# Memory attention with its factors made ahead: one token pipeline, and neighbourhood columns moved between the mLSTM

## The chip, the cores and the metric

The kernel runs on one core of a Trainium2 chip. The metric is the device time of one execution in microseconds; the median of several runs is given. The engines are named as the profile names them: PE (TensorE, matmuls), PEld (its weight loads), DVE (VectorE), ACT (ScalarE), POOL (GpSimd) and SP (SyncE, whose queue issues nearly all DMAs here).

## The reference, cut to what matters

One encoder layer over 1024 tokens of width 1024. Three sub-layers follow each other, each as x <- LayerNorm(alpha * x + f(x)): a token mixer (a bidirectional mLSTM with 4 heads of 128 beside a neighbourhood attention with 8 heads of 64), a cross-attention into 256 memory tokens, and a gated convolutional FFN. The change is in the cross-attention and in where the work around it stands.

```python
def memory_xattn(x, mem, w_q, w_kv, w_o, b_o):
    q = (x @ w_q).reshape(b, t, XA_HEADS, XA_DIM)          # 4 heads of 256
    k, v = jnp.split(mem @ w_kv, 2, axis=-1)               # each reshaped to (b, 256, 4, 256)
    s = jnp.einsum('bthd,bmhd->bhtm', q, k) * (XA_DIM ** -0.5)
    p = jax.nn.softmax(s, axis=-1)
    o = jnp.einsum('bhtm,bmhd->bthd', p, v).reshape(b, t, d)
    return o @ w_o + b_o
```

All inputs and outputs are fp32, and `w_q`, `w_kv`, `w_o` are 1024 rows deep.

## The kernel before, in words

**Precision.** A product is made of three matmuls (`mm3`, lines 220 to 222): each operand is a pair of a high part and a remainder, and high x high, high x low and low x high are summed in PSUM. Pairs are in fp32r (`wload`, `split`) in the mixer and in f16 with a power-of-two scale (`wload16`, `split16`, lines 196 and 197) from the cross-attention on. A weight comes by DMA into a `wraw` tile (two buffers), ACT makes `whi` from it, DVE or POOL makes `wlo` (five buffers each). The scales come from surveys of the weights and from bounds that are worked out on the chip.

**Order.** All engines run their own instruction streams. A tile framework orders each stream at build time, by program order and by its own simulated clock, and puts in the waits. A tile of a pool takes a buffer when an earlier tile of the same tag is free; pools that are opened after others were closed take over their memory. `mix(tc, anchor, main, total, fill, ftotal, lag)` interleaves two generators: after each step of `main` it takes steps of `fill`, in proportion, and holds them on each engine behind an instruction of `main` that is `lag` steps back.

**Stages.** (1) Tokens: eight tiles of x are normalized, transposed into `xT` (X1 for tokens 0 to 511, X2 for the rest) and multiplied with the token-major weights (`tok_chunk`); eight surveys of `w_xo` and `w_xq` run beside. (2) Columns: sixteen columns of `w_col`, each for both halves of the tokens, 32 groups of 24 matmuls (bank `cl`): q and k of the mLSTM, then q and k of the neighbourhood attention (stored to `nqk_d`). The gate scan and the backward state pass of the mLSTM run beside. (3) mLSTM (`ml_gen`), chunk by chunk; its fill is `mem_gen`: sixteen groups of 24 matmuls that make K (`xk_d`) and V (`xv_d`) of the 256 memory tokens. (4) Neighbourhood attention (`na_gen`), with the first half of the output product as its fill (`out_a`). The mLSTM's result `yml` lies in X1. (5) The second half of the output product (`out_half` with `after1`): norm, and `to_h1`, which transposes the normalized tile, applies the norm's weight and bias per partition and splits it into f16; POOL applies them to the row-major tile, which goes to `h1_d`. (6) The query projection `xq_gen` (16 groups of 24 matmuls; each column of `w_xq` is loaded and split twice, once for each half of the tokens) and the attention `attn` by head and half, with `load_kv` reading K and V back; the query projection is the fill. (7) `attn` goes on with the output product `out_d` as its fill; `w_xo` is loaded and split as `wD`. (8) The last four tiles of `out_d`, with the first units of the FFN being prepared (`units.bound`, `scale`, `prep`), and `to_B`, which makes the FFN's operands. (9) The FFN, then the down-projection.

## Time and profile before

| what | us |
|---|---|
| median of 3 runs (1615.37 to 1618.26) | 1616.17 |
| the profiled execution | 1614.52 |
| its span, first to last instruction | 1612.8 |
| PE busy in the span | 1500.4 |
| DVE busy | 1003.2 |
| ACT busy | 765.5 |
| POOL busy | 552.8 |

The mean granted clock of PE over the span is 0.976 of full speed. A row of a group reads: line, engine, operation, names of what is written and read, tile of the matmul, shape and type written and read, count, then busy time and mean of one in ns, then idle time of the engine just before and what ended it. PE's instructions overlap each other in the pipeline, so their busy times add up to more than the time they need; the distance from one start to the next is the pace.

### The profile page before, as it was taken

What the parts mean: (1) busy time and instruction counts of PE and PEld (TensorE: products, weight loads), DVE (VectorE), ACT (ScalarE), POOL (GpSimd) and SP (SyncE); (2) the same over time, 40 slices, a digit from 0 to 9 for tenths busy, and PEclk for the clock granted to TensorE, in tenths of its full rate; (3) what the DMA queues carried; (4) which work ended last, traced back from release to release, by engine and by line L of the source; (5) the groups of instructions that cost most, each with busy time, mean ns of one, the idle gap of its engine ahead of it and who ended that gap; (6) DMA issues with size and microseconds to landing.
All of it is one profiled execution on the core that took longest, in us unless ns stands there. A gap on an engine that the chain in (4) does not pass through costs nothing.

```text
span 1612.8 us, 21595 instructions
## 1 busy us (share of the span) xinstructions
PE 1500.4 (93%) x8132; PEld 974.6 (60%) x8132; DVE 1003.2 (62%) x1895; ACT 765.5 (47%) x1283; POOL 552.8 (34%) x373
## 2 busy tenths in 40 slices
PE   6999999999788999788899969999999999998998
PEld 6999888889777888544455434444444444443443
DVE  7413411136688785986675696877888877935333
ACT  3322211235566664545544477777777765611000
POOL 5414312123467661740000253633444410200442
PEclk9999999999999999899999979999999999998999
DMA  8255211255556424253311312323232333832011
GB/s 302 91 193 172 104 46 72 85 186 171 167 155 213 133 91 170 86 181 139 129 68 53 144 68 92 144 105 118 110 137 107 135 139 104 300 119 91 37 69 52
DMA packets 76345, 204.69 MB, mean 127 GB/s; under 512 B 7632, under 2 KB 26320, under 8 KB 73424
## 3 DMA queue, kind: packets, MB, share of 16 engines
q1 hardware_dynamic: 75952, 202.55, 35.6%
q8 instruction: 64, 1.05, 0.3%
q0 software_dynamic: 144, 0.49, 0.2%
q14 instruction: 41, 0.34, 0.1%
q10 hardware_dynamic: 144, 0.26, 0.0%
HBM read 160.71 MB, written 43.06 MB: 126 GB/s over the span
## 4 chain that ended last, share of the span: by engine, by line
PE 53%; DVE 19%; ACT 9%; DMA 8%; issue 3%; POOL 2%; SPq 0%; DVEq 0%; ACTq 0%; POOLq 0%
PE dn L222 5%; PE dn L221 5%; PE dn L220 5%; PE cl L222 4%; PE cl L220 4%; PE cl L221 4%; DVE cbuf L1320 3%; DVE wlo L197 3%; DVE cbuf L1321 2%; DMA sv<-in_w_down_dram 2%; PE tk L220 2%; PE tk L221 2%; PE tk L222 2%; DMA wraw<-in_w_xq_dram 2%; PE z L221 2%
## 5 line engine op out<-in xcount | busy, mean ns | idle before, releaser
L127 POOL TENSOR_TENSOR wlo<-wraw,whi 128x1024 fp32r<-128x1024 f32 (+1 forms) x36 | 86.6, 2414 | 197.9 <-ACT whi L126 194.5
L220 PE MATMUL dn<-whi,yp 128*128 128x512 f16 x336 | 127.4, 382 | 1.4 <-ACT whi L196 1.4
L221 PE MATMUL dn<-wlo,yp 128*128 128x512 f16 x336 | 128.4, 382 | 0.0
L222 PE MATMUL dn<-whi,yp 128*128 128x512 f16 x336 | 128.4, 382 | 0.0
L238 POOL TENSOR_TENSOR lnrs<-lnrs,mhalf 128x1 f32<-128x1 f32 x32 | 24.4, 762 | 270.0 <-DVE lnrs L237 259.4
L1239 POOL TENSOR_TENSOR wraw<-ur 128x512 f32<-128x512 f32 x22 | 45.8, 2080 | 190.5 <-issue 188.1
L126 ACT ACTIVATE whi<-wraw 128x1024 fp32r<-128x1024 f32 (+1 forms) x48 | 50.5, 1058 | 116.1 <-PE cl L221 67.6
L197 DVE SCALAR_TENSOR_TENSOR wlo<-wraw,sc,whi 128x1024 f16<-128x1024 f32 x45 | 66.5, 1494 | 47.7 <-ACT whi L196 47.6
L1320 DVE SCALAR_TENSOR_TENSOR cbuf<-C,wdw,cbuf 128x1024 f32<-128x1024 f32 x44 | 75.8, 1723 | 28.2 <-ACT cbuf L1319 28.1
L196 ACT ACTIVATE whi<-wraw,sc 128x1024 f16<-128x1024 f32 x45 | 50.7, 1144 | 76.6 <-PE dn L222 31.4
L1321 DVE SCALAR_TENSOR_TENSOR cbuf<-C,wdw,cbuf 128x1024 f32<-128x1024 f32 x44 | 70.5, 1601 | 1.2
L248 ACT ACTIVATE r<-r,lnrs 128x1024 f32<-128x1024 f32 x18 | 22.3, 1240 | 95.1 <-DVE lnrs L247 95.1
L220 PEld LDWEIGHTS <-yp 128*128 128x128 f16 x352 | 34.7, 98 | 51.7 <-issue 11.1
L221 PEld LDWEIGHTS <-whi 128*128 128x128 f16 x364 | 36.1, 99 | 47.3 <-issue 7.8
L222 PEld LDWEIGHTS <-wlo 128*128 128x128 f16 x364 | 36.0, 99 | 46.5 <-issue 6.0
L220 PEld LDWEIGHTS <-whi 128*128 128x128 f16 x364 | 36.0, 99 | 46.0 <-issue 4.3
L221 PEld LDWEIGHTS <-yp 128*128 128x128 f16 x352 | 34.7, 99 | 42.3 <-issue 1.4
L222 PEld LDWEIGHTS <-yp 128*128 128x128 f16 x352 | 34.7, 98 | 42.2 <-issue 1.1
L1319 ACT ACTIVATE cbuf<-C,bdw,wdw 128x1024 f32<-128x1024 f32 x44 | 54.5, 1238 | 10.7 <-DVE C L1356 9.6
L220 PE MATMUL tk<-whi,X2h 128*128 128x256 f32 (+1 forms) x192 | 55.4, 289 | 3.4 <-DVE ev L332 2.1
L220 PE MATMUL tk<-whi,X1h 128*128 128x256 f32 (+1 forms) x192 | 56.2, 293 | 1.2 <-DVE V L327 0.7
L222 PE MATMUL tk<-whi,X1l 128*128 128x256 f32 (+1 forms) x192 | 55.8, 292 | 0.4 <-DVE lnrs L237 0.4
(479 smaller groups left out, 4945.8 us busy)
## 6 DMA issues: line engine op xcount, KB each, us to landing
ur<-in_w_up_dram SPq DMA_DIRECT2D x22, 1024.0 KB
sv<-in_w_down_dram SPq DMA_DIRECT2D x22, 512.0 KB
y<-cbuf SPq DMA_DIRECT2D x22, 512.0 KB
ur<-y SPq DMA_DIRECT2D x11, 1024.0 KB
wraw<-in_w_down_dram SPq DMA_DIRECT2D x22, 512.0 KB
r<-h SPq DMA_DIRECT2D x19, 512.0 KB
wraw<-in_w_col_dram SPq DMA_DIRECT2D x16, 512.0 KB
wraw<-in_w_xq_dram SPq DMA_DIRECT2D x16, 512.0 KB
```

The source lines that it names most:

```text
L126: A.activation(hi[:, :n], r3, AF.Copy)
L127: (eng or G).tensor_tensor(lo[:, :n], r3, hi[:, :n].bitcast(F32), OP.subtract)
L196: A.activation(hi, src, AF.Copy, scale=s)
L197: return V.scalar_tensor_tensor(lo, src, s, hi, op0=OP.mult, op1=OP.subtract)
L220: T.matmul(ps, lh, rh, start=first, stop=False, skip_group_check=skip)
L221: T.matmul(ps, lh, rl, start=False, stop=False, skip_group_check=skip)
L222: return T.matmul(ps, ll, rh, start=False, stop=last, skip_group_check=skip)
L238: G.tensor_tensor(rs[:, 0:1], rs[:, 0:1], mhalf[:, 0:1], OP.pow)
L1239: G.tensor_tensor(S1, A21, A22, OP.add)
L1319: A.activation(c, C[:, 1:SEQ + 1], AF.Identity, scale=wdw[:, 1, j:j + 1], bias=bdw[:, j:j + 1])
L1320: V.scalar_tensor_tensor(c, C[:, 0:SEQ], wdw[:, 0, j:j + 1], c, op0=OP.mult, op1=OP.add)
L1321: V.scalar_tensor_tensor(c, C[:, 2:SEQ + 2], wdw[:, 2, j:j + 1], c, op0=OP.mult, op1=OP.add)
```

## The change

The cross-attention is written with its weights multiplied into the memory first. Scores of head h are x (Wq_h K_h') and the output is the sum over heads of P_h (V_h Wo_h). Both factors (1024 x 1024 each: 4 heads x 256 memory tokens against the width of 1024) are made in a stage of their own after the token stage and ahead of the columns: K and V as before, then `Kq` from the transposed `w_xq` and `Vo` from `w_xo`, each group split into an f16 pair and stored to DRAM (`kq_d`, `vo_d`). `wload16` with `pool=True`, for every second of these weights, makes the remainder with two POOL operations. After the mixer the pairs are read back as they are needed: `Kq` into the two tiles of the pool `yp`, `Vo` into four of the five `whi`/`wlo` buffers. One pipeline over the eight token tiles takes the place of stages 6 to 8: transpose and split (`to_hT`), scores and softmax of all four heads (`scores`), transpose of P (`to_PT`), output and norm (`out_d`). The norm's weight and bias are applied in the row-major tile (`ln_tile` with `lw`, `lb`), `to_h1` goes.

The columns of the mLSTM (8 columns, 16 groups) stay ahead of the mLSTM; the 8 columns of the neighbourhood attention (16 groups) become the mLSTM's fill in place of `mem_gen`. As X1 and X2 are then read until the end of the mLSTM, its result goes to DRAM (`yml_d`) and is read back and split in four pieces, and the first four output weights are loaded through `wraw` and no longer through X2. All eight surveys are maxima on DVE. In the way into the FFN the first unit's preparation is cut in other places.

```diff
-    def wload16(src, a, b, s):
+    def wload16(src, a, b, s, pool=False):
...
         S.dma_start(raw, src)
-        split16(hi, lo, raw, s)
+        if pool:
+            A.activation(hi, raw, AF.Copy, scale=s)
+            G.tensor_scalar(raw, raw, s, None, op0=OP.mult)
+            G.tensor_tensor(lo, raw, hi, OP.subtract)
+        else:
+            split16(hi, lo, raw, s)
...
+                ws = Stream([(I[w][i], 8, 128) for w in ("w_xk", "w_xv") for i in range(8)], 2, (V, None))
...
+                for j, name in enumerate(("xk", "xv")):
...
+                    for i in range(8):
+                        wh, wl = ws.get(8 * j + i)
+                        ps = bank("mem")[:, :256]
+                        for k in range(8):
+                            mm3(ps, wh[:, k, :], wl[:, k, :], mT[0][:, k, :], mT[1][:, k, :], k == 0, k == 7)
+                        A.activation(x[:, i, :], ps, AF.Copy)
+                        V.tensor_reduce(sums[:, 40 * j + i:40 * j + i + 1], x[:, i, :], axis=mybir.AxisListType.X,
+                                        op=OP.max, apply_absolute_value=True)
...
+                wq = Stream([(I["w_xqT"][i * 128:i * 128 + 128], 1, 1024) for i in range(8)] +
+                            [(I["w_xo"][i * 128:i * 128 + 128], 1, 1024) for i in range(8)], 2,
+                            load=lambda a, b, c, e: wload16(a, b, c, swq if wq.n < 8 else sx, wq.n % 2))
+
+                def stage(ps, dst, shape):
+                    st = mm.tile([128, 2, 512], F16, name="stage", tag="stage", bufs=4)
+                    split16(st[:, 0], st[:, 1], ps, 2.0 ** -23)
+                    for n in range(2):
+                        S.dma_start(dst(n), st[:, n].rearrange("p (a m) -> p a m", a=shape))
+
+                for h in range(4):
+                    w = [wq.get(2 * h), wq.get(2 * h + 1)]
+                    xh, xl = pairs["xk"]
+                    for j in range(4):
+                        ps = bank("mem")
...
+                        stage(ps, lambda n: kq_d[n, :, 2 * j:2 * j + 2, h * 256:h * 256 + 256], 2)
...
+                for h in range(4):
+                    w = [wq.get(8 + 2 * h), wq.get(9 + 2 * h)]
...
+                            stage(ps, lambda n: vo_d[n, :, 2 * h + b:2 * h + b + 1, c], 1)
...
-            todo = [(i, hf) for i in range(14) for hf in range(2)] + [(14, 1), (15, 1), (14, 0), (15, 0)]
+            todo = [(i, hf) for i in (4, 5, 6, 7, 0, 1) for hf in range(2)] + [(2, 0), (3, 0), (2, 1), (3, 1)]
+            for n, _ in enumerate(col_gen(todo)):
...
-                    split(yml[0][:, :, cs], yml[1][:, :, cs], pt)
+                    A.activation(hm, pt, AF.Copy)
+                    S.dma_start(yml_d[c].rearrange("p (h t) -> p h t", h=4), hm)
...
-            mg = mem_gen()
-            next(mg)
-            mix(tc, anchor, ml_gen(), 48.3, mg, 14.5, 3)
+            cg = col_gen([(i, hf) for p in range(4) for i in (8 + p, 12 + p) for hf in range(2)])
+            next(cg)
+            mix(tc, anchor, ml_gen(), 48.3, cg, 15, 3)
...
-        wA = out_w("w_mix_out", 0, (None, V, None, V), oraw)
+        wA = out_w("w_mix_out", 0, (None, V, None, V))
+        yml = tuple(t.rearrange("p (k t) -> p k t", k=4) for t in slot("X1"))
+        for c in range(0, NT, 2):
+            raw = wp.tile([128, WP], F32, name="wraw", tag="wraw", bufs=2)[:, :D]
+            S.dma_start(raw.rearrange("p (c x) -> p c x", c=2), yml_d[c:c + 2].rearrange("c p x -> p c x"))
...
+        def to_hT(ck, n):
+            r = rs[n]
+            hT[n] = ck.tile([128, 2, 8, 128], F16, name="h1T", tag="h1T", bufs=2)
...
+            G.tensor_tensor(r, r, bxo, OP.add)
+
+        def scores(ck, n):
+            t = hT.pop(n)
+            P = ck.tile([128, D], F32, name="P", tag="P", bufs=1)
+            for ch in range(2):
+                ps = bank("S2")
+                for k in range(8):
+                    c = slice(ch * 512, ch * 512 + 512)
+                    mm3(ps, t[:, 0, k], t[:, 1, k], Kq[0][:, k, c], Kq[1][:, k, c], k == 0, k == 7)
...
+            return P
...
+        def out_d(n, lag=1):
+            r, t, tt = rs.pop(n), probs.pop(n), todo[n]
+            for ch in range(2):
+                ps = bank("S2")
+                c = slice(ch * 512, ch * 512 + 512)
+                for k in range(8):
+                    mm3(ps, t[:, 0, k], t[:, 1, k], Vo[0][k][:, c], Vo[1][k][:, c], k == 0, k == 7)
+                V.scalar_tensor_tensor(r[:, c], r[:, c], alx, ps, op0=OP.mult, op1=OP.add)
+                yield
+            holds.append(ln_tile(r, None, None, small, hold=holds[-1] if holds else None, late=n == NT - 1, eps=epx))
+            S.dma_start(h2_d[tt * 128:(tt + 1) * 128, :], r)
...
+            for n in range(NT):
+                Pn = scores(ck, n + 1) if n + 1 < NT else None
+                to_PT(P, n)
+                P = Pn
+                if n + 2 < NT:
+                    load_r(n + 3)
+                    to_hT(ck, n + 2)
+                if 0 < n < NT - 1:
+                    run(out_d(n - 1))
```

472 lines of the change are left out of this document (192 added, 280 removed).

## The prediction

> **What bounds the kernel now.** I read the page's busy times and slices first, then the busy times by stretch, then the spacing of matmuls inside the stretches, and last the waits.
>
> ```profile
> PE 1500.4 (93%) x8132; PEld 974.6 (60%) x8132; DVE 1003.2 (62%) x1895; ACT 765.5 (47%) x1283; POOL 552.8 (34%) x373
> PE   6999999999788999788899969999999999998998
> PEclk9999999999999999899999979999999999998999
> ```
>
> TensorE holds the span; no other engine passes 62%. So the time is TensorE's work at its full pace plus what it stands idle or runs at a halved clock. The stretches, cut where the stages change:
>
> ```profile
> 0.00:173.00 173.00, 155.74 (x1224) 152.30 (x1225) 80.77 (x164) 50.10 (x65) 64.84 (x52) 0.99 0.52 186
> 173.00:360.00 187.00, 187.00 (x872) 154.82 (x872) 41.00 (x89) 34.04 (x74) 41.66 (x25) 1.00 0.27 94
> 360.00:471.40 111.40, 98.12 (x792) 95.90 (x792) 74.94 (x286) 65.16 (x167) 51.29 (x36) 0.95 0.57 166
> 471.40:632.00 160.60, 144.67 (x922) 127.61 (x921) 124.77 (x358) 102.82 (x284) 98.67 (x94) 0.99 0.43 145
> 632.00:720.00 88.00, 71.85 (x332) 47.80 (x332) 74.59 (x118) 39.85 (x69) 46.76 (x24) 0.90 0.38 132
> 720.00:820.00 100.00, 88.39 (x463) 47.60 (x462) 64.07 (x143) 53.33 (x101) 0.00 (x0) 0.93 0.41 148
> 820.00:895.00 75.00, 75.00 (x409) 40.71 (x408) 45.34 (x127) 30.68 (x71) 2.25 (x4) 1.00 0.13 50
> 895.00:980.00 85.00, 72.71 (x330) 34.94 (x329) 68.92 (x122) 52.90 (x81) 42.05 (x36) 0.90 0.31 113
> 980.00:1612.80 632.80, 606.94 (x2802) 272.89 (x2799) 428.83 (x494) 336.57 (x376) 205.23 (x103) 0.99 0.31 116
> ```
>
> Columns: stretch, its length, then busy time and count of PE, PEld, DVE, ACT, POOL, then granted clock. In order: tokens; columns; mLSTM with the memory projections as fill; neighbourhood attention; output half with the start of the query projection; query projection with attention; attention with the output; the way into the FFN; the rest. A matmul's busy time overlaps its neighbours', so work is counted by spacing:
>
> ```profile
> 220.00:240.00 20.00, 20.00 (x90) 16.56 (x89) 2.25 (x3) 1.06 (x1) 4.21 (x2) 1.00 0.16 53
> 80.00:100.00 20.00, 20.00 (x169) 20.00 (x168) 2.97 (x7) 4.69 (x5) 0.77 (x1) 1.00 0.57 193
> 1000.00:1020.00 20.00, 20.00 (x95) 9.15 (x94) 18.01 (x22) 16.57 (x22) 10.27 (x6) 1.00 0.36 133
> 800.16 0.27 PE L220 MATMUL S<-kh,pYl 128*128 128x256 f16 x1
> 800.27 0.27 PE L221 MATMUL S<-kl,pYl 128*128 128x256 f16 x1
> ```
>
> These give 0.228 us for fp32r of 512 columns, 0.119 for 256 (edge instructions taken off), 0.215 for f16 of 512, 0.11 for f16 of 256. Stretch 632 to 720 holds
>
> ```profile
> L220 PE MATMUL out<-whi,X2h 128*128 128x512 f32 x49 | 19.4, 395 | 1.3 <-ACT X2h L225 1.3
> L220 PE MATMUL xq<-pX1h,whi 128*128 128x512 f16 x32 | 13.7, 435 | 4.7 <-DVE pYh L197 4.7
> L957 PE MATMUL tp<-ident,r 128*128 128x128 f32 x64 | 9.6, 293 | 6.6 <-DVE t L917 3.5 <-ACT t L915 3.1
> ```
>
> with three matmuls to each of the first two rows and 24 more of f16: 147 x 0.228 + 120 x 0.215 + 64 x 0.11 = 66 us in 88, so 22 lost. Counted the same way, the loss is 22 us in the mLSTM, 25 in neighbourhood attention, 17 in 720 to 820, none in 820 to 895, 19 in 895 to 980.
>
> **The work does not change.** Scores 8x2x24 = 384 f16 matmuls of 512 replace the query projection's 384; the factor Wq K' (4x4x2x2x3 = 192 of 256) replaces the old scores' 192; V Wo (96 of 512) the old P V's 96. Output products, memory projections, columns and transposes keep their counts. What moves is where TensorE waits, so I cost the change stage by stage in lost time.
>
> **Tokens: +2 (0 to +8).** Four 1 MB surveys go from ACT to DVE:
>
> ```profile
> 160.00 2.29 DVE L206 TENSOR_REDUCE sums<-sv 128x1 f32<-128x2048 f32 x1 [4.75 <-DMA sv<-in_w_xq_dram]
> 162.67 0.58 PE L220 MATMUL tk<-whi,X2h 128*128 128x256 f32 x1 [2.07 <-DVE ev L332]
> ```
>
> One such reduction held up an eviction and TensorE for 2.07 us. A chunk takes 24 x 0.119 = 2.86, so mostly a reduction hides; four stalls would be 8.
>
> **The factors, now alone on TensorE: +22 (+10 to +42).** The memory projections, 384 x 0.119 = 46 us, were mLSTM fill; with the factors (192 x 0.11 + 96 x 0.215 = 42) they become a stage with no other work under it. Its 16 raw factor weights pass through two wraw buffers:
>
> ```profile
> 798.24 3.18 DMA wraw<-in_w_xo_dram
> L196 ACT ACTIVATE whi<-wraw,sc x18: 1137/1148/1168, 730.1 to 809.4; 128x1024 f16<-128x1024 f32 x18
> L197 DVE SCALAR_TENSOR_TENSOR wlo<-wraw,sc,whi x17: 1276/1284/1285, 731.2 to 808.4; 128x1024 f16<-128x1024 f32 x17
> L197 DVE SCALAR_TENSOR_TENSOR wlo<-wraw,sc,whi 128x1024 f16<-128x1024 f32 x5 | 11.9, 2387 | 0.0
> L127 POOL TENSOR_TENSOR wlo<-wraw,whi 128x1024 fp32r<-128x1024 f32 x35 | 84.1, 2411 | 191.4 <-ACT whi L126 188.0 <-issue 2.8 <-POOL whi L550 0.6
> L1051 POOL TENSOR_TENSOR wlo<-r,whi 128x512 f16<-128x512 f32 x4 | 7.4, 1856 | 11.6 <-ACT whi L1050 11.6
> L800 POOL MEMSET qsh<- 128x512 f32 x2 | 1.1, 528 | 0.0
> L196 ACT ACTIVATE pYh<-xq,sc 128x512 f16<-128x512 f32 x4 | 2.7, 684 | 5.2 <-PE xq L222 5.2
> L197 DVE SCALAR_TENSOR_TENSOR pYh<-xq,sc,pYh 128x512 f16<-128x512 f32 x4 | 3.0, 741 | 2.2 <-ACT pYh L196 2.2
> ```
>
> An even weight holds its buffer 3.18 + 1.15 + 1.28 = 5.7 us, or 6.8 where DVE's split runs beside POOL (2387 ns in the stretch from 632). An odd one is scaled and subtracted on POOL. No row shows POOL scaling 1024 elements: between two memsets (1.06) and a two-input pass (2.41); the subtraction to f16 lies between 2.41 and twice 1.86 = 3.7. So odd holds 7.8 to 10.4, I take 9.1. Each load takes the buffer that is free, so a pair costs (6.8 + 9.1)/2 = 8.0 us; it could be 6.8, or 10.4 if the buffers alternate strictly. A pair feeds 48 x 0.11 or 24 x 0.215 = 5.2 us of TensorE; eight pairs lose 8 x 2.8 = 22. Ends: 8 x 1.6 less a pair or so loaded ahead is 10, 8 x 5.2 = 42. The projections before them need 2.86 us a weight against 5.9 to 6.8 us in two buffers, a deficit covered by the weights loaded during the token stage, so nothing. ACT and DVE also split 32 results (0.68 + 0.74 each), four to a pair: with the weights' splits 5.0 us of ACT and 4.2 to 5.4 of DVE a pair, below the 8; the 64 stores of 128 KB, eight to a pair, go out on SP's queue between the weight loads and can delay those, which is in the upper end. The stage leaves DRAM 8 MB to store and 8 MB to read back as finished pairs; the reads land under the output half, 16 x 12 x 0.228 = 44 us long.
>
> The Trainium skill ("GPSIMD Engine Reference", section 3.1) puts a one-input POOL pass at 1.03 cycles an element and a two-input one at 2.6; an estimate from it is 0.9 + 2.2 us for the two steps, an odd hold of 7.4. The two-input figure agrees with the 2.41 us row, the f16 rows run slower; no run here shows the one-input case. By that page the pair would be 7.1, this stage +15, the whole 1596.
>
> **Columns: +1.** Sixteen of 32 column groups stay in front of the mLSTM, 5.5 us each, as before without loss; 1 us for the entry.
>
> **mLSTM: -13 (-18 to -5).** The fill becomes 16 groups of 24 x 0.228 = 5.5 us instead of 16 of 2.86, 42 us more work into 22 us of waits such as
>
> ```profile
> L674 PE MATMUL num<-V,whi 128*128 128x129 f32 x128 | 24.3, 282 | 5.0 <-ACT hm L686 5.0
> PE tp L715 <- DVE hm L712: 3.6, 2, 2.1
> ```
>
> These are the mLSTM's own chain and remain, but a fill twice as long runs through most of them. ACT and DVE lose 8 of the 16 weight splits there. I keep 9 lost.
>
> **Entry to neighbourhood attention: +3 (-3 to +12).** X1 and X2 stay occupied until the last column group, so the four output weights, and the mLSTM output (stored, read back and split in four pieces), now go through wraw ahead of r and kr: some eight uses. About half can land before the mLSTM ends; the last piece waits for a store and a load (2 x 3.2) and a split of 2.5, 9 us, and kr lands 3.2 later. TensorE has two tiles of output product, 11 us, against that.
>
> **Output half and token pipeline: -27 (-33 to -10).** Lost between 632 and 895 now: 22 + 17 = 39. Three causes are removed:
>
> ```profile
> L961 DVE TENSOR_TENSOR pX1h<-t,pX1h 128x512 f16<-128x512 f32 x8 | 13.3, 1659 | 0.5 <-ACT pX1h L960 0.5
> L962 POOL TENSOR_TENSOR r<-r,vec 128x1024 f32<-128x1024 f32 x8 | 20.9, 2606 | 15.2 <-PE tp L957 12.3 <-issue 1.6 <-ACT t L915 1.3
> L251 DVE TENSOR_TENSOR r<-r,vec 128x1024 f32<-128x1024 f32 x4 | 6.1, 1537 | 5.2 <-ACT r L248 5.2
> ACT whi L196 <- DMA wraw<-in_w_xo_dram: 10.6, 7, 3.5
> 808.99 0.37 PE L220 MATMUL S<-kh,pYl 128*128 128x256 f16 x1 [7.36 <-ACT P L1083]
> 809.37 0.42 PE L222 MATMUL S<-kh,pYl 128*128 128x256 f16 x1
> 809.59 0.42 PE L220 MATMUL S<-kh,pYl 128*128 128x256 f16 x1
> ```
>
> DVE, full between 660 and 700, works against POOL; ACT stands in order behind weight loads while the exponential waits; after the 7.36 us gap TensorE runs at half pace (0.22 instead of 0.11 apart). Afterwards no raw weight is loaded or split here. Per tile TensorE has 96 x 0.215 + 24 x 0.11 = 23 us; the work beside it is that of 820 to 895, where DVE was busy 60% and ACT 41% and nothing was lost. The norm's full form (one more DVE pass of 1.54 us as L251 and a POOL addition of 2.6 as L962) fits in the 5.5 us a tile of the output half, the bias (one such addition a tile) in the 23. I leave 2 for the output half, 5 until the first tile's operands are written (their memory is the r buffers of the stage before, which wait for tile 5's norm and store), 5 for the single P buffer and the two transpose banks: 2 + 5 + 5 = 12. One loss of 3.4 us in each tile would be 8 x 3.4 = 27 more, the same as before.
>
> **Into the FFN: -1 (-8 to +8).** Same products, norms and unit splits; the units' home is free earlier, P and Vo last longer.
>
> **Sum.** 2 + 22 + 1 - 13 + 3 - 27 - 1 = -13. The profiled execution took 1614.5 (span 1612.8), so 1601.5 by itself; the median of the three runs, 1616.2, is 1.7 above it: **1603**.
>
> **Rivals.** (A) The two wraw buffers decide, and it ends slower. A pair of P us loses 8 x (P - 5.2); above P = 9.6 that exceeds the 35 saved net elsewhere. With 11 us (strict alternation at 10.4, 64 stores slowing the loads) it is 46, time 1627. For it: the loads' 3.18 us was measured at 148 GB/s, here the pair moves 2 MB. Against: the buffers are free to swap. Chance 0.27. (B) The new waits hide: weights ahead cover the factors to +10, the mLSTM saves 18, the pipeline 32: 2 + 10 + 1 - 18 + 3 - 32 - 1 = -35, 1581. For it: 820 to 895 without loss. Chance 0.18. (C) The saving does not arise: the factor stage takes what the pipeline gives (P near 9.6, or 1.6 us a tile stay), 1616. Chance 0.12. My forecast, 1591 to 1611, has 0.43.
>
> **How the numbers follow.** A measurement here can tell some 0.2%, 3.2 us, from no change. Faster is forecast and B: 0.61; same is C: 0.12; slower is A: 0.27. The range runs from just below B to A: 1580 to 1630; beside it the likeliest case's own 1591 to 1611.
>
> **What would show it.** Right: a factor stage of some 110 to 115 us with TensorE waiting on wlo from POOL or on wraw loads; mLSTM with columns near 140 us; a token pipeline with PE above 95% busy at full clock; no wait on wraw loads there. Wrong: a factor stage under 95 or over 130; TensorE idle 2 us or more in each token tile, on P or a transpose bank; a start of neighbourhood attention that waits over 15 us for kr or the read-back.

## The result, and the profile after

The changed kernel takes 1665.51 us (median; 1660.96 to 1666.28), the kernel before 1617.11 beside it: ratio 1.0294, 95% interval 1.0273 to 1.0316. It is slower by 48 us, where 13 us faster was forecast. The profiled execution, the shortest of the four, took 1660.96 us with a span of 1659.2.

The page's busy times and slices of the changed kernel, then its stretches (columns as in the prediction):

```profile
PE 1504.0 (91%) x8134; PEld 973.1 (59%) x8134; DVE 969.2 (58%) x1774; ACT 734.7 (44%) x1212; POOL 584.3 (35%) x389
PE   6999786799999589895999988999999999998998
PEclk9999898999999799997999999999999999999999
...
173.00:235.00 62.00, 51.26 (x377) 49.10 (x377) 32.77 (x69) 25.01 (x35) 19.35 (x8) 0.89 0.47 153
235.00:316.00 81.00, 55.75 (x319) 33.66 (x319) 34.98 (x53) 36.77 (x54) 42.09 (x17) 0.92 0.59 191
316.00:419.70 103.70, 103.28 (x504) 86.23 (x503) 23.67 (x51) 23.54 (x53) 27.48 (x15) 1.00 0.28 91
419.70:555.00 135.30, 129.20 (x767) 112.71 (x765) 67.01 (x258) 57.65 (x155) 50.00 (x42) 1.00 0.49 145
555.00:590.00 35.00, 12.69 (x42) 9.59 (x42) 17.64 (x40) 10.54 (x22) 13.97 (x17) 0.66 0.47 155
...
732.00:767.00 35.00, 34.09 (x153) 28.24 (x154) 22.92 (x52) 5.36 (x5) 9.98 (x8) 1.00 0.42 158
767.00:980.00 213.00, 188.33 (x949) 95.85 (x947) 110.14 (x240) 77.15 (x156) 48.17 (x32) 0.94 0.20 75
```

The matmuls are as many as before (8134 against 8132), so the work is what was forecast; the 48 us are waiting. It lies in the projections (173 to 235), the factors (235 to 316), the start of the neighbourhood attention (555 to 590) and the start of the token pipeline (767 on). Columns, mLSTM and output half run at full clock. The timeline names what TensorE waited for at these places (start, duration, instruction, in brackets the idle time before it and what ended it), and SyncE's queue beside them:

```profile
177.35 0.58 PE L223 MATMUL mem<-memTh,whi 128*128 128x256 f32 x1 [6.56 <-ACT whi L127]
567.02 1.11 PE L755 MATMUL tp<-ident,hm 128*128 128x128 f32 x4 [7.57 <-DVE hm L752]
578.95 0.79 PE L223 MATMUL fill<-whi,X1h 128*128 128x512 f32 x1 [10.82 <-DVE wraw L796]
586.51 1.22 PE L223 MATMUL S<-kh,qsh 128*128 128x256 f32 x3 [2.70 <-ACT kh L885]
789.94 0.61 PE L223 MATMUL S<-kq,h1T 128*128 128x512 f16 x1 [22.27 <-ACT h1T L202]
...
164.98 6.80 SPq L342 DMA_DIRECT2D mo<-ev  x3
172.86 1.47 SPq L126 DMA_DIRECT2D wraw<-in_w_xk_dram  x2
570.93 0.37 SPq L811 DMA_DIRECT2D wraw<-yml  x1
571.92 0.37 SPq L779 DMA_DIRECT2D wraw<-h  x1
580.15 0.60 SPq L865 DMA_DIRECT2D wraw<-nqk  x1
```

The gap at 568 to 579 needs the two kinds of rows together. DVE's addition into the first output tile (L796) ended it, and it waited for r0 (`wraw<-h`), which SP could issue only at 571.92, behind the last read-back of the mLSTM's result; with one PSUM bank for this fill TensorE can't go on. k of the first heads (`wraw<-nqk`) came 8 us later still. The 7.57 us gap ahead of it ended on the mLSTM's last norm (L752).

Stage by stage, TensorE's lost time (length less matmuls times spacing, as in the prediction), after less before, against the forecast:

| stretch | forecast | measured |
|---|---|---|
| tokens | +2 | 0 |
| projections and factors | +22 | +53 |
| columns | +1 | 0 |
| mLSTM | -13 | -12 |
| start and rest of the neighbourhood attention | +3 | +16.5 |
| output half and token pipeline | -27 | -9 |
| into the FFN | -1 | -2 |
| sum | -13 | +46 |

### The profile page after: what moved, and what is told of

It is laid out like the page before. It is cut to its first block, busy times and chain, and to the rows that moved or that the text cites. A ratio compares the mean times of both kernels' runs of the same rounds, so it can differ in the third digit from the quotient of the medians.

```text
span 1659.2 us, 21607 instructions
## 1 busy us (share of the span) xinstructions
PE 1504.0 (91%) x8134; PEld 973.1 (59%) x8134; DVE 969.2 (58%) x1774; ACT 734.7 (44%) x1212; POOL 584.3 (35%) x389
## 4 chain that ended last, share of the span: by engine, by line
PE 29%; DVE 11%; ACT 6%; DMA 3%; issue 1%; POOL 1%; SPq 0%; DVEq 0%; ACTq 0%
PE dn L224 5%; PE dn L225 5%; PE dn L223 5%; PE S L223 3%; PE S L224 3%; PE S L225 3%; DMA sv<-in_w_down_dram 3%; DVE cbuf L1299 2%; DVE cbuf L1300 2%; PE z L224 1%; PE z L225 1%; PE z L223 1%; ACT cbuf L1298 1%; ACT cbuf L1306 1%; DVE wlo L203 1%
## 5 line engine op out<-in xcount | busy, mean ns | idle before, releaser
L128 POOL TENSOR_TENSOR wlo<-wraw,whi 128x1024 fp32r<-128x1024 f32 (+1 forms) x38 | 91.3, 2407 | 198.9 <-ACT whi L127 176.0
L127 ACT ACTIVATE whi<-wraw 128x1024 fp32r<-128x1024 f32 (+1 forms) x52 | 54.9, 1060 | 148.8 <-PE tk L225 47.9
L251 ACT ACTIVATE r<-r,lnrs 128x1024 f32<-128x1024 f32 x19 | 23.6, 1241 | 121.6 <-DVE lnrs L250 121.6
L223 PE MATMUL S<-kq,h1T 128*128 128x512 f16 x128 | 49.5, 387 | 22.6 <-ACT h1T L202 22.6
L223 PEld LDWEIGHTS <-yp 128*128 128x128 f16 x352 | 34.5, 98 | 51.4 <-issue 10.4
L203 DVE SCALAR_TENSOR_TENSOR wlo<-wraw,sc,whi 128x1024 f16<-128x1024 f32 x29 | 43.5, 1521 | 31.4 <-ACT whi L202 31.3
L1075 POOL TENSOR_TENSOR r<-r,vec 128x1024 f32<-128x1024 f32 x8 | 18.8, 2348 | 113.1 <-PE tp L1073 113.1
L202 ACT ACTIVATE whi<-wraw,sc 128x1024 f16<-128x1024 f32 x29 | 32.4, 1142 | 58.6 <-PE dn L225 33.3
L224 PE MATMUL tk<-wlo,X1h 128*128 128x256 f32 (+1 forms) x192 | 55.3, 289 | 0.0
L225 PE MATMUL tk<-whi,X2l 128*128 128x256 f32 (+1 forms) x192 | 54.7, 285 | 0.0
```

The costliest lines, as they stand in the source:

```text
L127: A.activation(hi[:, :n], r3, AF.Copy)
L128: (eng or G).tensor_tensor(lo[:, :n], r3, hi[:, :n].bitcast(F32), OP.subtract)
L202: A.activation(hi, src, AF.Copy, scale=s)
L203: return V.scalar_tensor_tensor(lo, src, s, hi, op0=OP.mult, op1=OP.subtract)
L223: T.matmul(ps, lh, rh, start=first, stop=False, skip_group_check=skip)
L224: T.matmul(ps, lh, rl, start=False, stop=False, skip_group_check=skip)
```

## The experiments: the factor stage

The changed kernel's 1665.5 us and 1.0294 are what each result is held against; line numbers are those of the kernel shown.

A part of some of these differences lies outside the edited stage. From the start of the last score matmul to the end of the span, the profiled executions of e5, e10, e12, e14 and c6 take 677.7 to 678.7 us, those of the other changed kernels 681.0 to 684.4. No edit touches the FFN, most of that stretch, but in these five ACT and DVE run its instructions in another order than in the changed kernel, as the framework orders the streams anew at each build. So some 4 us of the gain of each of the five come from there. That the order alone does it isn't shown: e4 has the order of e5 and takes 681.2.

The theory: each weight passes through one of two raw buffers, and POOL's two passes hold one too long. Groups of the changed kernel from 235 to 316 (line, engine, operation, tiles, count, busy us, mean ns, idle time before and its causes), then POOL beside DVE in its timeline:

```profile
L137 POOL TENSOR_SCALAR wraw<-wraw,sc 128x1024 f32<-128x1024 f32 x8 | 22.8, 2847 | 41.5 <-ACT whi L136 28.3 <-PE mem L224 7.6 <-DMA wraw<-in_w_xqT_dram 5.6
L138 POOL TENSOR_TENSOR wlo<-wraw,whi 128x1024 f16<-128x1024 f32 x8 | 17.9, 2236 | 0.7
L203 DVE SCALAR_TENSOR_TENSOR wlo<-wraw,sc,whi 128x1024 f16<-128x1024 f32 x7 | 11.8, 1692 | 0.3 <-ACT whi L202 0.3
L136 ACT ACTIVATE whi<-wraw,sc 128x1024 f16<-128x1024 f32 x8 | 9.2, 1147 | 13.9 <-DMA wraw<-in_w_xo_dram 11.6 <-DMA wraw<-in_w_xqT_dram 2.3
```

```profile
260.99 2.12 POOL L138 TENSOR_TENSOR wlo<-wraw,whi 128x1024 f16<-128x1024 f32 x1
261.21 2.98 DVE L203 SCALAR_TENSOR_TENSOR wlo<-wraw,sc,whi 128x1024 f16<-128x1024 f32 x1
```

ACT's splits of the odd weights start at 236.46 first and 308.26 last, eight of them, 10.26 us apart in the mean (7.4 to 12.7). Load 3.2, ACT 1.15, POOL 2.85 and 2.24 make 9.4 of it. That is near the prediction's end for strict alternation (10.4), not the 8.0 it took, but the buffers don't alternate strictly. SyncE's queue shows it (two loads; then its waits ahead of all these loads: us in total, times, longest):

```profile
264.22 0.34 SPq L134 DMA_DIRECT2D wraw<-in_w_xqT_dram  x1
264.67 0.38 SPq L134 DMA_DIRECT2D wraw<-in_w_xo_dram  x1
...
SPq L134 <- POOL wlo L138: 9.3, 3, 5.8
SPq L134 <- DVE wlo L203: 8.6, 7, 2.2
```

The load at 264.22 is that of an odd weight, the last of `w_xqT`. It goes out when DVE's split of the even weight ahead of it has ended (264.19), although POOL has been done with the odd one since 263.11; the even weight behind it takes POOL's buffer. So it is from the sixth weight on. Both holds are longer than assumed. From the issue of its load to the end of its last pass an even weight held its buffer for 8.1 to 10.9 us (mean of seven 9.1; the prediction took 6.8), an odd one for 9.5 to 11.2 (10.1; it took 9.1): DVE's split stands in DVE's order behind the splits of results, and in three of seven cases it ended 1.08 us after POOL's subtraction. The factor products, first to last, take 81 us for 42 of work.

**POOL's passes taken away (e3).**

```diff
-                            load=lambda a, b, c, e: wload16(a, b, c, swq if wq.n < 8 else sx, wq.n % 2))
+                            load=lambda a, b, c, e: wload16(a, b, c, swq if wq.n < 8 else sx))
```

> One edit: all sixteen factor weights are split by ACT and DVE, none by the two POOL passes. Theory (two raw buffers in strict turn, the odd one held by POOL): the odd weights follow each other 10.26 us apart now (load 3.2, ACT 1.15, POOL 2.85 and 2.12, issue about 1); without POOL the cycle is 3.2 + 1.15 + 1.28 + 1 = 6.6 for either buffer, so eight pairs gain 8 x 3.5 = 28 us less what DVE's eight more splits (10 us in all) hold up: 15 to 26 us less, kernel 1640 to 1650. Rival (loads delayed by the 64 stores in the same queue, or by DMA rate): the cycle stays near 10, less than 5 us. Rival (DVE becomes the bound, splits of results wait): 5 to 12 us less.

Measured: 1646.22 us, ratio to before 1.0186 (1.0153 to 1.0219), 19 us below the changed kernel; the factor products take 58 us. So POOL's passes are what holds the weights up; neither the 64 stores nor DVE keeps the pair at 10 us:

```profile
L203 DVE SCALAR_TENSOR_TENSOR wlo<-wraw,sc,whi 128x1024 f16<-128x1024 f32 x15 | 19.2, 1282 | 11.4 <-ACT whi L202 11.2
```

DVE's split is back at 1.28 us from a mean of 1.69.

**POOL's passes given to both buffers in turn (e4).**

```diff
-                            ... swq if wq.n < 8 else sx, wq.n % 2))
+                            ... swq if wq.n < 8 else sx, wq.n % 4 in (1, 2)))
```

> One edit: the POOL passes are kept for eight of the sixteen factor weights, but for those whose number modulo four is 1 or 2 instead of every odd one, so that each of the two raw buffers is in turn held long and short. Theory (strict turn): a buffer now takes 10.3 + 6.6 us for two pairs instead of 20.6, 8.5 a pair: 8 x 1.8 = 14 us less, 9 to 16, kernel 1650 to 1657. Rival (the buffers are taken as they come free, or POOL's own rate of 4.97 us a weight or the shared stores decide): no change, 1665 within 3.

Measured: 1666.91, ratio 1.0309 (1.0278 to 1.0340): no change, a miss. The edit puts two POOL weights next to each other, and POOL then holds both buffers at once (9.9 to 11.2 us of POOL in a row for a pair of weights):

```profile
239.96 2.85 POOL L137 TENSOR_SCALAR wraw<-wraw,sc 128x1024 f32<-128x1024 f32 x1 [6.04 <-ACT whi L136]
243.10 2.84 POOL L137 TENSOR_SCALAR wraw<-wraw,sc 128x1024 f32<-128x1024 f32 x1 [0.28 <-ACT whi L136]
245.91 5.53 POOL L138 TENSOR_TENSOR wlo<-wraw,whi 128x1024 f16<-128x1024 f32 x2
```

So it doesn't test the turn by itself, and its premise, that every odd weight has the same buffer, doesn't hold in the changed kernel.

**Six raw buffers, POOL kept (e5).** Two of every three pairs of weights pass through the halves of `memT`, which is free after the projections.

```diff
+                def fraw(i):
+                    if i // 2 % 3 == 0:
+                        return None
+                    if i % 2 == 0:
+                        n = "hl"[i // 2 % 3 - 1]
+                        fr[0] = mm.tile([128, 8, 256], F32R, name="memT" + n).bitcast(F32).rearrange("p a b -> p (a b)")
+                    return fr[0][:, i % 2 * 1024:i % 2 * 1024 + 1024]
...
+                            load=lambda a, b, c, e: wload16(a, b, c, swq if wq.n < 8 else sx, wq.n % 2, raw=fraw(wq.n)))
```

> One edit: the factor weights pass through six raw buffers (the two of wraw and the halves of the two memT tiles, free after the projections) instead of two; POOL's two passes for every odd weight stay. Theory (a raw buffer is held too long, 10.3 us by an odd weight): loads are ahead, an odd weight costs POOL 4.97 us a pair and DVE, ACT stay below, so a pair takes 5.5 to 7: 240 to 316 shrinks by 15 to 25 us, kernel 1641 to 1651. Rival (POOL's passes and the order on the engines decide, not the buffers: DVE's split of the even weight waits for POOL, the odd remainder comes 5 us after its high part): less than 6 us, kernel 1660 to 1666.

Measured: 1642.37, ratio 1.0162 (1.0147 to 1.0177), 23 us less, 18 of them by the last factor product; factors 59 us. POOL's passes are no shorter (3.06 us for L137 on `memTh`).

**Both (e14).**

> e3 and e5 together: six raw buffers and no POOL passes for the factor weights. The factor products took 81 us in the changed kernel, 58 with POOL's passes gone (e3) and 59 with the buffers (e5), for 42 us of TensorE's work. Theory (POOL's passes cost by the time for which they hold one of two buffers, and nothing else): with six buffers it doesn't matter who splits, so this run is the same as e5 within 4 us: 1638 to 1646. Rival (POOL's passes also cost as such, by the late remainder or by slowing DVE beside them): another 5 to 12 us less, 1630 to 1637.

Measured: 1639.75, ratio 1.0134 (1.0117 to 1.0151); factors 57.6 us. That is 3 us below e5 and 6 below e3, inside the theory's range. At the last score matmul, ahead of the FFN, e14 and e3 are level (959.4 us), and e5 is 4.2 behind them (963.6). So either cure alone gives most of it: of the 18 us by which e3 is ahead of the changed kernel there (977.1), POOL's passes cost some 4 as such and the rest by keeping two buffers busy. Of TensorE's 9.5 us of idle time in the factors of e14, 7.2 ended on DVE's split of a result (`stage`; the two longest gaps 2.5 and 2.7 us), the rest on weights.

## The experiments: the entry of the stage

**Memory tokens early, four raw buffers (e10).** The memory tokens come into the two `vec` tiles that the token norm has left, two weights are loaded ahead, and every second pair of projection weights passes through tiles that the pair of V takes later.

```diff
+                    if c == 4:
+                        for q in range(2):
+                            mraw.append(vecs.tile([128, D], F32, name=f"vec{q}", tag=f"vec{q}").rearrange(
+                                "p (k t) -> p k t", k=4))
+                            S.dma_start(mraw[q], I["memT"][:, q * 1024:(q + 1) * 1024].rearrange("p (k t) -> p k t", k=4))
...
+                    if c == 5:
+                        wm = Stream([(I[w][i], 8, 128) for w in ("w_xk", "w_xv") for i in range(8)], 2, (V, None))
+                        wm.load_next()
+                        wm.load_next()
...
+                ws = wm
+                ws.load = lambda a, b, c, e: wload(a, b, c, e, None if ws.n % 4 < 2 else mm.tile(
+                    [128, 8, 256], F16, name="xv" + "hl"[ws.n % 2]).rearrange("p a b -> p (a b)").bitcast(F32))
```

> Two edits at the entry of the new stage, read in two stretches: (1) the memory tokens come early into the two vec tiles that the token norm has left, not through wraw, and the first two projection weights are loaded before the last token chunk's stores; (2) the sixteen projection weights pass through four raw buffers (two of them tiles that the later pair of V takes) instead of two. Theory: (1) the gap of 6.56 us at 170.8 is the wait for the first weight, issued at 172.86 behind the memory tokens' splits and the stores; it falls to 0 to 2; (2) 11 us lost from 182 to 240 are loads: two buffers held 5.9 to 6.8 us give one weight in 3.4 us against 2.86; with four it falls to 0 to 4. Together 10 to 17 us less, kernel 1649 to 1656. Rival: ACT and DVE (or POOL's 2.4 us for every odd remainder, 192 of the 384 matmuls' operands) set 3.4 us a weight, and the gap moves to the memory tokens' splits at 171.6: 0 to 5 us less.

Measured: 1648.11, ratio 1.0195 (1.0176 to 1.0214), 17 us less. The same two stretches in the changed kernel (first two rows) and in e10:

```profile
169.00:182.00 13.00, 4.67 (x20) 4.19 (x21) 5.51 (x10) 4.42 (x5) 2.85 (x2) 0.67 0.43 134
182.00:240.00 58.00, 52.07 (x403) 49.69 (x403) 32.02 (x75) 26.17 (x40) 19.46 (x9) 0.96 0.44 147
```

```profile
169.00:182.00 13.00, 9.71 (x65) 9.12 (x64) 6.53 (x11) 5.53 (x7) 1.74 (x2) 0.87 0.30 104
182.00:240.00 58.00, 53.23 (x435) 50.59 (x434) 40.91 (x80) 27.16 (x43) 27.92 (x11) 0.97 0.44 145
```

77 more matmuls are done by 240. The 6.56 us gap is gone, and the projections' 11 us fall to 8, less than the theory said.

## The experiments: the start of the neighbourhood attention

**r0 and kr ahead of the read-back (e8).**

```diff
+        r0 = wp.tile([128, WP], F32R, name="whi", tag="whi", bufs=5).bitcast(F32)[:, :D]
+        S.dma_start(r0, h0_d[0:128, :])
+        kr0 = wp.tile([128, WP], F32R, name="wlo", tag="wlo", bufs=5).bitcast(F32)[:, :D]
+        S.dma_start(kr0, nqk_d[4])
         yml = tuple(...slot("X1"))
```

> One edit: the residual of the first output tile (r0) and k of the first pair of heads (kr) are loaded into the fifth whi and wlo buffers, ahead of the read-back of the mLSTM's result, instead of through wraw behind it. Theory (wraw and SP's queue): TensorE's gap of 10.8 us at 568 is the wait for r0, issued at 571.92 behind the last read-back and landing at 578, and the 2.7 us at 584 is kr, issued at 580.15; both go, the tail of the mLSTM (7.6 us at 559) stays: 10 to 13 us less, kernel 1652 to 1656. Rival (the last read-back itself): the second output tile and the first scores then wait for the last piece of the mLSTM's result (stored at 568.8, loaded, split) or for DVE, and the gap reappears there: 0 to 4 less.

Measured: 1657.46, ratio 1.0259 (1.0244 to 1.0275), 8 us less, between theory and rival. The gaps of 7.6 and 10.8 us are gone; the mLSTM's last norm ends no earlier (569.6 against 567.0), but the output product, which now has its r0, runs ahead of it:

```profile
555.00:590.00 35.00, 23.45 (x102) 18.41 (x101) 26.37 (x67) 17.39 (x40) 20.36 (x21) 0.85 0.47 158
```

102 matmuls instead of 42 in these 35 us; TensorE still waits 2.7 us for DVE's addition into the first output tile and 3.3 us for the split of q.

## The experiments: the 22 us ahead of the token pipeline

ACT, DVE and POOL in the changed kernel, around the last two norms (power L241, factor L250, ACT's pass L251, DVE's L254, POOL's bias L255, statistics L236):

```profile
782.23 1.24 ACT L251 ACTIVATE r<-r,lnrs 128x1024 f32<-128x1024 f32 x1 [4.47 <-DVE lnrs L250]
783.50 1.23 DVE L254 TENSOR_TENSOR r<-r,vec 128x1024 f32<-128x1024 f32 x1 [1.31 <-ACT r L251]
784.64 1.28 DVE L236 BATCH_NORM_STATS2 lnst<-r 128x6 f32<-128x512 f32 x2
784.80 2.34 POOL L255 TENSOR_TENSOR r<-r,vec 128x1024 f32<-128x1024 f32 x1 [2.86 <-DVE r L254]
787.10 0.55 POOL L241 TENSOR_TENSOR lnrs<-lnrs,mhalf 128x1 f32<-128x1 f32 x1
787.93 1.24 ACT L251 ACTIVATE r<-r,lnrs 128x1024 f32<-128x1024 f32 x1 [4.47 <-DVE lnrs L250]
789.20 1.27 ACT L202 ACTIVATE h1T<-tp,sc 128x512 f16<-128x512 f32 x2
```

A norm every 5.7 us, each after the one before, and the first split of the new pipeline behind the last. My first theory was the hold: the next tile's statistics are tied behind L254. The rival was memory: `h1T` lies over r buffers of the output half.

**Shorter hold (e1, first cut); memory of its own, in a pool opened before `wkB` (e2, second cut).**

```diff
-        a = V.tensor_tensor(r, r, w_t, OP.mult)
+        V.tensor_tensor(r, r, w_t, OP.mult)
         G.tensor_tensor(r, r, b_t, OP.add)
-        return a
+        return n
```
```diff
+        cC = ExitStack()
+        ck = cC.enter_context(tc.tile_pool(name="wkC", bufs=1, reuse_waits="tile"))
...
-        with ExitStack() as cC:
-            ck = cC.enter_context(tc.tile_pool(name="wkC", bufs=1, reuse_waits="tile"))
+        with cC:
+            pass
```

> One edit: the held norm of the output half is released by the norm's small DVE instruction (the scale times mean) instead of the later multiplication with the norm's weight, so that the next tile's statistics need not wait for ACT's pass. Theory (norm chain): in the changed kernel the norms follow each other 5.7 to 7.1 us apart, one whole serial chain each, against 5.46 us of TensorE a tile, so they finish 22 us after the last product; ACT takes the split of the first h1T behind the last norm. With the short hold a norm takes some 3 to 4.5 us of chain, the eighth ends soon after its product, and the gap of 22.28 us before the first scores shrinks to 5 to 9: kernel 1648 to 1654, 12 to 18 us below 1665.5. Rival (memory): h1T lies over r buffers of tiles 5 and 6 and waits for their stores; since the stores come earlier with the shorter chain too, it gives a gain, but by those stores' landing (some 2 us each after the norm) a gap of 10 or more stays. Rival (something else on TensorE's side, such as the loads of h1 or Kq): gap unchanged, 1665 within 3.

> One edit: the tiles of h1T and P get memory of their own, opened before the output half, so that they no longer lie over its r buffers; the hold is left as it is. Theory (norm chain, ACT in order): the split of the first h1T still stands behind the last norm on ACT, so nothing moves: gap 22 us within 1, kernel 1665 within 3. Rival (memory): the split goes as soon as its transposes are done, at about 768, and the gap falls to 3 to 6 us: kernel 1647 to 1651.

Measured: e1 1665.10, ratio 1.0304 (1.0272 to 1.0337), gap 22.2 us: a miss. e2 1674.71, ratio 1.0369 (1.0332 to 1.0406), gap 32.4 us, and not for either reason: the transposes now wait for the load of h1 itself, which SP issues only at 795.08, behind the output half's last store (issued at 792.64). By the pools' sizes its tiles overlap the output half's r buffers in this layout (argued, not shown), so e2 moved the wait and says nothing of the split.

```profile
799.02 1.33 PE L1073 MATMUL tp<-ident,r 128*128 128x128 f32 x5 [32.36 <-DMA r<-h]
```

e1 shows why the hold isn't alone: POOL's addition waits for DVE's pass, and the next tile's power stands behind it on POOL. That is a second loop of the same length (0.55 + 0.21 + 1.24 + 1.2 + 2.34, with the releases 5.7).

**The addition behind the power (e9, e11).** In e9 it was only issued later in the program; the framework's own order put it back ahead of the next power (in the trace addition at 775.61, power 777.90, addition 781.31), so e9 repeats e1. In e11 it is tied there, and the bias addition and the store (`finish`) go out one tile later (the cut is e11's).

```diff
+                if tt > 0:
+                    with tc.issue_after(pows[-1].ins):
+                        finish(*rl.pop(0))
```

> Two edits in the output half: the short hold as in e1, and POOL's addition of the norm's bias (2.34 to 2.40 us) with the store is issued one tile later, behind the next tile's power instead of ahead of it. Theory (POOL in order): in e1 the norms still followed each other 5.7 to 6.5 us apart, because the next tile's power on POOL stood behind this tile's addition, which waits for ACT (1.25) and DVE (1.2); the loop power 0.55, factor 0.2, ACT 1.25, DVE 1.2, POOL 2.35 gives 5.7. With the addition behind, the loop is 0.55 + 0.2 + 1.25 + 1.2 + 0.15 and releases, 4 us, under the 5.46 of TensorE: the eighth norm ends some 6 us after the last product, the gap falls from 22.3 to 6 to 10, kernel 1649 to 1655. Rival (memory): the first h1T waits for the store of tile 5 or 6, which now goes out later than the norm of tile 7 by 2.4 + 2 us: gap 11 to 15, kernel 1654 to 1660. Rival (neither): unchanged, 1665 within 3.

> What e9 was meant to do: in e9 the addition still stood ahead of the next tile's power on POOL (the trace shows addition, power, addition, power, each pair 5.70 us after the last). Here each addition is tied behind the next tile's power on POOL. Theory (POOL's place in the loop): the loop of one norm is then power 0.55, factor 0.21, ACT 1.24, DVE 1.18, sum 0.15 and releases, some 3.5 to 4.3 us, under TensorE's 5.46 a tile; the eighth norm's ACT pass ends 5 to 8 us after the last product instead of 21.5, the gap falls from 22 to 7 to 12 and the half clock behind it shortens: 10 to 17 us less, kernel 1649 to 1656. Rival (memory: h1T waits for the stores of tiles 5 and 6): the gap stays above 14. Rival (DVE's whole work of the stage is the bound): DVE does 16 residual additions of 0.69 and eight times 1.28 + 0.36 + 0.21 + 1.18, 35 us in the 44 of the products: it would leave the gap at 10 to 14 too, but with DVE busy without a break.

Measured: e9 1664.01, ratio 1.0292 (1.0275 to 1.0310), gap 21.9 us. e11 1658.34, ratio 1.0253 (1.0234 to 1.0271): 7 us less, gap 16.2 us, the memory rival's number.

**Norms on DVE alone (e12).**

```diff
-                holds.append(ln_tile(r, lw, lb, small, hold=holds[-1] if holds else None))
+                ln_tile(r, lw, lb, small, late=True)
```

> The norms of the output half in the other form that the kernel has: DVE does both passes (subtract and multiply by the weight, multiply and add the bias), no ACT pass, no POOL addition, no hold. Theory (chain over ACT, DVE, POOL): the chain has gone; ACT is free for the split of h1T at 768, and DVE's work a tile is 2 x 0.69 + 1.28 + 0.36 + 2 x 1.24 = 5.5 us, TensorE's own pace, so DVE ends some 5 to 10 us after the last product: gap 8 to 13, kernel 1653 to 1659. Rival (memory): gap 14 or more, as the stores of tiles 5 and 6 must have gone. Rival (DVE too full, residuals late): TensorE stands in the output half itself and nothing is won, 1662 to 1668.

Measured: 1652.02, ratio 1.0209 (1.0184 to 1.0234), 13 us less, gap 14.1 us. In both, ACT now waits for the stores that free the memory (first row e11, second e12):

```profile
786.66 1.27 ACT L202 ACTIVATE h1T<-tp,sc 128x512 f16<-128x512 f32 x2 [5.46 <-DMA h<-r]
```

```profile
778.69 1.26 ACT L202 ACTIVATE h1T<-tp,sc 128x512 f16<-128x512 f32 x2 [48.14 <-DMA h<-r]
```

**The first tile moved, the norms left (e13).** The pool `hp`, from which h1T comes now, is opened ahead of `wkB`.

```diff
+        hp = cH.enter_context(tc.tile_pool(name="hT", bufs=1, reuse_waits="tile"))
...
                 S.dma_start(h1_d[tt * 128:(tt + 1) * 128, :], r)
+                if tt == 3:
+                    load_r(0)
+                if tt == 5:
+                    to_hT(None, 0)
...
-            run(out_half(wB, ylk(yna), part0_d, None, wk, "out", after1, rbufs=5))
...
+            run(out_half(wB, ylk(yna), part0_d, None, wk, "out", after1, rbufs=4))
```

> The norm chain of the output half is left exactly as it is in the changed kernel (5.7 to 7.1 us a tile). Only the first token tile's operand is moved: h1T gets memory of its own (the output half's r buffers go from five to four to make room), and the load, the transposes and the split of the first tile are issued after the sixth of the eight output tiles, so that on ACT and DVE they stand behind the sixth norm and not behind the last. Theory (what the gap waits for is the place of the first split, behind all norms in ACT's and DVE's order and behind the stores that free its memory; the chain's length matters only through that): TensorE goes from the last product into the scores, 10.3 us of work per tile, while the last norms end; gap 22 to below 3, and no half clock behind it: 18 to 24 us less, kernel 1641 to 1648. Rival (the norms' length itself holds up the pipeline): the wait moves to the next consumer of DVE, the maximum and exponentials of the first scores or the second tile's split, and 5 to 12 us are won.

Measured: 1653.01, ratio 1.0230 (1.0211 to 1.0249), 12.5 us less, 5 us short of the theory's 1641 to 1648. The gap falls to 2.84 us, as the theory said, but the rival's wait appears too: ACT takes the exponentials of the first scores behind the last norm, and TensorE stops for 3.5 us.

```profile
765.74 1.26 ACT L202 ACTIVATE h1T<-tp,sc 128x512 f16<-128x512 f32 x2 [1.04 <-PE tp L983]
797.81 1.24 ACT L251 ACTIVATE r<-r,lnrs 128x1024 f32<-128x1024 f32 x1 [4.74 <-DVE lnrs L250]
798.96 0.55 ACT L1100 ACTIVATE P<-S,mn,sc 128x256 f32<-128x256 f32 x1
...
803.35 1.94 PE L1115 MATMUL tp<-ident,P 128*128 128x128 f32 x8 [3.50 <-DVE P L1105]
```

So the two causes are both there: the place of the first split, and the form of the norms. The next kernels have both cures.

## The experiments: together

c3 is e10, e5, e8 and e11; c5 has e13 in place of e11; c6 is c5 with e12's norms; c7 is c6 without POOL's passes.

> The edits that gave something together: early memory tokens and four raw buffers for the projections (e10, 17 us less), six raw buffers for the factor weights with POOL's passes kept (e5, 23 less), r0 and kr of the first pair ahead of the read-back (e8, 8 less), and the addition behind the power (e11, 10 to 17 less if its theory holds, else 0). If the stages' losses add up: 1665 - 48 - (10 to 17) = 1600 to 1607, ratio to before 0.990 to 0.995; without e11's part 1615 to 1620. If the loss moves on instead of going (weights late elsewhere, DRAM or SP's queue): above 1625.

> e10, e5, e8 and e13 together: 1665.5 - 17 - 23 - 8 - (18 to 24) = 1593 to 1600, below the kernel before, ratio 0.986 to 0.990, if the losses of the stages are independent, as c3 suggests (48 expected without its last part, of which 43 to 45 came). If e13's rival holds: 1604 to 1612.

> c5 with the norms of the output half done by DVE alone (the form of e12). Theory (place of the first split): the same as c5 within 3, since the norms then run beside the scores in either form. Rival (norm length): another 3 to 8 below c5.

> c6 with no POOL passes for the factor weights. By the same theory the same as c6 within 3 (1599 to 1605); by its rival 1590 to 1597.

| kernel | us | ratio to before |
|---|---|---|
| c3 | 1622.64 | 1.0045 (1.0029 to 1.0060) |
| c5 | 1616.44 | 1.0000 (0.9984 to 1.0016) |
| c6 | 1602.31 | 0.9914 (0.9898 to 0.9931) |
| c7 | 1604.50 | 0.9919 (0.9904 to 0.9933) |

c6 is 63 us below the changed kernel and 0.9% below the kernel before. c3 met neither 1600 to 1607 nor 1615 to 1620: it is 43 us below the changed kernel, where the single gains add up to 55. c5 missed its forecast by 16 to 23 us, on three counts. e10 and e5 don't add up: the last factor product ends at 301 with e10, 298 with e5 and 291 with both, against 316 (25 us, not the 33 of the two alone). Their 17 and 23 us hold 7 more that lie behind the factors. And e13 gave 12.5 us, not the 18 to 24 that were written in.

The last score matmul starts at 931.8 in c5, 923.2 in c6 and 918.9 in c7. So of the 14 us between c5 and c6 the norms' form is worth 8.6, with the first split moved in both; that is the rival's side, just above its 3 to 8. The other 5.5 lie behind it. c7 came out level with c6, as the theory said, but by luck: its last factor product ends at 284 and not 291, it is still 4.3 us ahead at the scores, and the stretch behind them takes 6.0 longer. Ahead of the FFN, then, POOL's passes cost some 4 us even with six buffers, as e14 against e5 showed. The pipeline of c6:

```profile
703.00:738.00 35.00, 34.50 (x157) 28.57 (x157) 28.27 (x57) 1.64 (x3) 8.78 (x6) 1.00 0.48 168
738.00:926.00 188.00, 185.62 (x944) 94.89 (x943) 110.31 (x235) 70.84 (x149) 38.95 (x26) 1.00 0.22 82
```

188 us at full clock instead of the 213 above; 3.7 lost instead of 28.7. Not settled is what holds the 32 us that c6 still loses from 169 to 291; no run took the split of the results away.

## Why the prediction was wrong, step by step

- **mLSTM, -13:** right, -12. The longer fill covers the chain's waits; 9.5 us stay lost, 9 were forecast. Columns, tokens and the way into the FFN came within 2 us. The token pipeline, once it runs, loses nothing, as the rows from 820 to 895 of before said.
- **Factors, +22:** the term failed in its two holds. "Each load takes the buffer that is free" came true from the sixth weight on, and the average of the measured holds, (9.1 + 10.1)/2 = 9.6, comes near the pair's 10.26. But the odd weight held 10.1 us and not 9.1: the scaling pass on POOL, bounded by 1.06 and 2.41 us, took 2.85, above both ends. And the even weight held 9.1 and not 6.8, as its split waits in DVE's order and behind POOL. Eight pairs at 10.26 less 5.2 would have been 40; measured, 35 to 39, inside the term's own +10 to +42.
- **"So nothing" for the projections:** failed by 18 us, 7 at the entry and 11 in the stage. The weights that were to be loaded during the token stage weren't: the memory tokens took both buffers, and SP issued the first weight at 172.86. The 2.86 against 3.4 us a weight then showed in full.
- **Neighbourhood attention, +3:** the queue was counted rightly (some eight uses of wraw), its effect wasn't. The two tiles of output product that should have covered it need r0, and r0 stood in the same queue: 16.5 us. e8 took 8 of them back.
- **Pipeline, "5 until the first tile's operands are written":** 22 and a cold clock behind it. The named cause (memory of the r buffers) was one of two; the order behind the last norm on ACT and DVE wasn't seen, nor that the norm's full form makes a serial loop of 5.7 us over ACT, DVE and POOL. It was costed by its parts (1.54 and 2.6 us "fit in the 5.5 us a tile"), as load and not as the length of a chain. c6, with both cures, loses 3.7 us in the pipeline where the changed kernel loses 28.7.
- **The signs named for a wrong forecast:** the first came, projections and factors took 143 us where 130 was the limit. The neighbourhood attention waited 13.5 us at its start for r0 and k, under the 15 named, and 21 with the gap ahead of them.
- **Rival A** named the right side, and its pair of 10.4 us lies near the measured 10.26, but not for its reasons: the buffers are not in strict alternation, and e3 keeps the 64 stores. Its 1627 holds the factor stage alone: the three other misses (18, 13.5 and 18 us) lie beyond it. They are also what the range of 1580 to 1630 had no room for: the projections' loss was put at nothing, and the neighbourhood attention (+16.5, upper end +12) and the pipeline (-9, upper end -10) lie past the ends of their own terms.

By the Trainium skill ("GPSIMD Engine Reference", section 3.1) the scaling pass was estimated at 0.9 us and the whole at 1596. The 2.85 us row goes against it, three times over; its two-input figure agrees with L138's 2.12 to 2.24 us.

## What to carry to other kernels

A stage moved out from under other work needs its supply priced as a chain: every use of a shared buffer with its whole hold, which takes in the waits of each pass in its engine's order, and every load in the order in which the queue can issue it. At a border between two stages look for the first instruction of the new one in each engine's order, and at whose memory it takes; work that "fits" by its busy time still delays it by its length. Two loops of equal length hide each other: shortening one showed nothing (e1) until the other was cut too (e11). And where a framework orders the streams at each build, compare two kernels stage by stage: an edit here can move some us in a stage that it doesn't touch.

## What the runs showed of the hardware

- POOL's scaling of 128x1024 f32 by a per-partition scalar took 2.85 us, longer than its subtraction of two tiles (2.12).
- DVE's split, 1.28 us alone, ends 1.08 us after POOL's subtraction when both want to run: POOL ends at 252.49 and 263.11, DVE at 253.57 and 264.19. Where DVE starts first POOL waits: with a split from 271.45 to 272.73 the subtraction took 3.03 us (271.68 to 274.71). Beside POOL's scaling pass (289.46 to 292.30) it isn't so: the split at 290.92 took 1.28 us, as alone. The Trainium skill ("SBUF — State Buffer", "SBUF: two separate sides") calls the port that the two share an exclusive lock; the rows of the subtraction agree, that of the scaling pass does not.
- After the 22 us gap TensorE runs at half clock for some 4 us more (clock of the changed kernel by 2 us):

```profile
790.00:792.00 2.00, 2.00 (x5) 0.66 (x6) 1.75 (x3) 0.46 (x1) 1.49 (x1) 0.50 0.00 0
792.00:794.00 2.00, 2.00 (x6) 0.73 (x5) 0.00 (x0) 0.00 (x0) 0.86 (x1) 0.50 0.19 72
794.00:796.00 2.00, 2.00 (x9) 0.83 (x8) 0.00 (x0) 0.00 (x0) 0.00 (x0) 0.86 0.49 199
796.00:798.00 2.00, 2.00 (x11) 0.88 (x9) 0.00 (x0) 0.00 (x0) 0.00 (x0) 1.00 0.00 0
```

In c5 a gap of 3.5 us was enough for the same (clock 0.50 from 766 to 772). So a wait of a few microseconds can cost 2 to 3 more. It doesn't always: behind a gap of 2.7 us in c5, which ends at 490.21, the clock stays at 1.00 (490 to 494).
